# A decoder layer on one core: the 32x32 diagonal blocks of a half inverted in one pass of steps instead of two, in a PSUM bank

## The chip, the cores and the metric

The kernel runs on one core of a Trainium2 chip. The metric is the device time of one execution in microseconds (us), as the median of several runs; a profiled execution stands beside them. The engines are named as in the profile: PE is TensorE, DVE is VectorE, ACT is ScalarE, POOL is GpSimd, SP is SyncE, which issues most DMAs. SBUF is the on-chip memory with 128 partitions, PSUM the accumulation memory with eight banks of 512 fp32 numbers per partition.

## What is computed

One layer of a hybrid decoder over 1024 tokens of 1024 numbers: an input projection, sliding-window attention for one group of heads, a gated DeltaNet for four other heads, an output projection, an MLP and a gated embedding `p @ w_ple_proj`. The change lies in the DeltaNet. Its chunked form needs, for each chunk of 64 tokens and each head, the inverse of a lower triangular matrix with ones on its diagonal:

```python
L = jnp.where(strict, jnp.einsum('bhncd,bhnsd->bhncs', k_beta, k) * decay, 0.0)
eye = jnp.eye(C, dtype=q.dtype)                       # C = 64
T = lax.linalg.triangular_solve(eye + L, jnp.broadcast_to(eye, L.shape),
                                left_side=True, lower=True)
u = jnp.einsum('bhncs,bhnsd->bhncd', T, v_beta)
w = jnp.einsum('bhncs,bhnsd->bhncd', T, k_beta * jnp.exp(g)[..., None])
```

and then a scan over the chunks with a state per head. `p @ w_ple_proj` depends on nothing of the layer, and is used only at its end.

## The kernel before

The 1024 tokens are two halves of 512, each of four token tiles of 128. Matmuls in fp32 are made of three passes of a rounded format, for which each weight tile is split: ScalarE rounds it (L219), VectorE or GpSimd subtracts (L220).

**How the order comes about.** The program is written as Python generators: a long filler (`projections`, L1083 on, PE's large matmuls) and tasks (`prepare`, `attend`, `chain`, `pairs`) that are woken by events and by due times in a count of PE time. That gives the order in which instructions are written down. The scheduler of the framework then makes a fixed order for each engine, by a model of the durations and with that order as the priority. On the chip each engine works off its own queue in that order and waits by semaphores. `take(k)` (L157) gives a PSUM bank of a ring: "g" has three for large matmuls; "d" has four and "e" one in the first stage, two and three afterwards (L1187).

**The recurrence's part.** `chain(hb, ...)` (L1170) runs for each half: `scalars`, `norms` (the scale `bb` of the blocks goes to a DRAM buffer BD and comes back as `bS`, L702 to L705) and `pre` (L717). For each token tile, `pre` makes the decay (POOL `rD` L722, ACT `et` L733, POOL L735), two products per head on PE, and multiplies them by `et` into `ka` (DVE, L749). The 32x32 diagonal blocks of the first product go to a DRAM buffer LD (L755). After tile 1 and after tile 3 it calls `inverse(s, g)` (L760) for a group of two tiles.

`inverse` handles 32 blocks (2 tiles x 4 heads x 4 blocks). The 128 partitions are 32 blocks x 4 parts of 8 columns of the inverse. It zeroes XS and sets ones (POOL, L769 and L773), loads LS, the blocks (SP, L772, four DMAs), scales LS by `bS` (DVE, L775) and takes 31 steps of forward substitution. A step is a product into `tp` (L779) and a subtraction from XS (L780), both on DVE over (31 - j) x min(j + 1, 8) elements a partition; each needs the instruction before it. Then XS goes to a DRAM buffer XD (SP, L782, four DMAs). Group 0 has tiles LS and XS of its own, group 1 uses the tiles `rD` and `et` again, which are free after the last tile's `ka`. The two groups' steps can be in flight at the same time.

`merge(s, tt)` (L784), one per token tile, begins when both groups of the half have been written down: `load_x` brings the inverses from XD into Xt (two buffers, SP, L839), DVE transposes them (L800), and PE and DVE join pairs of 32x32 inverses to 64x64. `prep` and `scan` follow, the scan with two groups of heads and a state `St`; its results `oS` (L947) go to PE to be transposed (L106).

**What PE has beside it.** In the second half of the stage PE's filler is the last projection, then `embed` (L1047, `p @ w_ple_proj`, 192 matmuls of 128x256, started as a spare while the first half's scan is awaited), then `w_out(0)` (384 such matmuls), which needs the first half's scan but nothing of the second half, then `w_out(1)`, the first part of which needs no scan.

Of the kernel before, what the change touches and what calls it, by code (L numbers as in the profile page):

```python
# [10 lines left out]
F32 = mybir.dt.float32  # L11
F32R = mybir.dt.float32r
AF = mybir.ActivationFunctionType
ALU = mybir.AluOpType
# [4 lines left out]
P = 128  # L19
# [90 lines left out]
def bc(ap, dim, n):  # L110

    a = ap.unsqueeze(dim)
    shape = list(a.shape)
    shape[dim] = n
    return a.to_broadcast(shape)
# [3 lines left out]
def hybrid_block(ctx, tc, t, out):  # L119
# [493 lines left out]
    def dt_(shape, name, p=dn, bufs=None, dt=F32):  # L613
        return p.tile(shape, dt, tag=name, name=nm(name), bufs=bufs)
# [51 lines left out]
    def norms(s, q, k):  # L666

        b, free = yield from take("e")
        sq = dt_([P, 2, 4, P], "rD", bufs=1, dt=F32R).bitcast(F32).rearrange("p i h c -> p i (h c)")
        xs = [(sel[i], x[:, h, 3:], h) for i, x in enumerate((q, k)) for h in range(4)]  # L670
        for j in range(9):
            if j < 8:
                A.activation(sq[:, j % 2], xs[j][1], AF.Square)
                yield 0.99
            if j:
                m, _, h = xs[j - 1]
                T.matmul(b[h * 32:h * 32 + 32, :], m, sq[:, (j - 1) % 2],
                         start=j <= 4, stop=j > 4)
        sb = dt_([P, 4, P], "et", bufs=1).rearrange("p h c -> p (h c)")
        A.copy(sb, b)  # L680
        free()
        yield 2.38
        b, free = yield from take("e")
        for tt in range(4):
            T.transpose(b[:, tt * P:(tt + 1) * P], sb[:, tt * P:(tt + 1) * P], ident)
        for i in range(2):
            V.tensor_scalar(s["ss"][:, i].rearrange("p (t h) -> p t h", t=4),
                            b.rearrange("p (t h x) -> p x t h", t=4, h=4)[:, i], EPS, None,
                            op0=ALU.add)
        free()  # L690
        w = lambda name: dt_([P, 16], name, bufs=2)
        rk2, rk, c2d, cc, bb = w("rk2"), w("rk"), w("c2d"), w("cc"), w("bb")
        ssq, ssk = s["ss"][:, 0], s["ss"][:, 1]
        V.reciprocal(rk2, ssk)
        V.tensor_tensor(bb, s["beta"], rk2, op=ALU.mult)
        yield 3.17
        b, free = yield from take("e")
        T.transpose(b[0:16, 0:P], bb, ident)
        bT = dt_([16, P], "bT", bufs=1)
        A.copy(bT, b[0:16, 0:P])  # L700
        free()
        SY.dma_start(s["BD"], bT)  # L702
        bS = dt_([P, 2, 32], "bS")
        for x in range(4):
            SY.dma_start(bS[x * 32:x * 32 + 32], s["BD"].rearrange("(g x) (b c) -> (x b) g c", g=2, b=4))  # L705
        G.tensor_tensor(rk, ssk, mhalf, op=ALU.pow)
        sc4 = dt_([P, 4, 2, 2, 2], "sc4", bufs=2)
        v = lambda x: x.rearrange("p (t g h) -> p t g h", t=4, g=2)
        V.tensor_tensor(sc4[:, :, :, 0], v(bb), v(s["eG"]), op=ALU.mult)
        V.tensor_tensor(sc4[:, :, :, 1], v(s["beta"]), v(rk), op=ALU.mult)  # L710
        V.reciprocal(c2d, ssq)
        V.tensor_scalar(c2d, c2d, 1.0 / (128.0 * 128.0), None, op0=ALU.mult)
        G.tensor_tensor(cc, ssq, mhalf, op=ALU.pow)
        V.tensor_scalar(cc, cc, 128.0 ** -0.5, None, op0=ALU.mult)
        s.update(bb=bb, bS=bS, sc4=sc4, c2d=c2d, cc=cc)

    def pre(s, q, k, place):  # L717
# [10 lines left out]
        for tt in range(4):  # L728
            b, free = yield from take("e")
            for i in range(2):  # L730
                T.matmul(b, mgtR, rD[:, i].rearrange("p h c -> p (h c)"), start=i == 0, stop=i == 1)
            et = dt_([P, 4, P], "et", bufs=1)
            A.activation(et, b.rearrange("p (h c) -> p h c", h=4), AF.Exp)  # L733
            free()
            G.tensor_tensor(et, et, bc(mle, 1, 4), op=ALU.mult)  # L735
            if tt < 3:
                rD = decay(tt + 1)
            kap, wait = place(tt)
            for e in wait:
                yield e  # L740
            ka = dt_([P, 2, 4, P], "ka", kap, bufs=4 if kap is dn else 2)
            s["KE"][tt], s["AT"][tt] = ka[:, 0], ka[:, 1]
            sl = slice(3 + tt * P, 3 + (tt + 1) * P)
            yield 3.0
            for j, x in enumerate((k, q)):
                b, free = yield from take("e")
                for h in range(4):
                    T.matmul(b[:, h * P:(h + 1) * P], k[:, h, sl], x[:, h, sl], start=True, stop=True)
                V.tensor_tensor(ka[:, j], b.rearrange("p (h c) -> p h c", h=4), et, op=ALU.mult)  # L749
                free()  # L750
                if j == 0:
                    ld = s["LD"].rearrange("(t h b) (s c) -> t b s h c", t=4, h=4, s=32)
                    for blk in range(4):
                        r = slice(blk * 32, blk * 32 + 32)
                        SY.dma_start(ld[tt, blk], ka[r, 0, :, r])  # L755
                yield 3.02
            if tt % 2:
                inverse(s, tt // 2)

    def inverse(s, g):  # L760


        if g:
            LS = dt_([P, 2, 4, P], "rD", bufs=1, dt=F32R).bitcast(F32).rearrange("p i h c -> p (i h c)")
            XS = dt_([P, 4, P], "et", bufs=1).rearrange("p h c -> p (h c)")[:, 0:256]
        else:
            LS, XS = dt_([P, 1024], "LS", bufs=1), dt_([P, 256], "XS", bufs=1)
        y = slice(g * 32, g * 32 + 32)
        G.memset(XS, 0.0)  # L769
        for x in range(4):  # L770
            d = slice(x * 32, x * 32 + 32)
            SY.dma_start(LS[d], s["LD"][y])  # L772
            G.memset(XS[d, x * 8:256:33], 1.0)  # L773
        LS, X3 = LS.rearrange("p (s c) -> p s c", s=32), XS.rearrange("p (j i) -> p j i", j=8)
        V.tensor_tensor(LS, LS, bc(s["bS"][:, g], 1, 32), op=ALU.mult)  # L775
        for j in range(31):
            n, m = 31 - j, min(j + 1, 8)
            tp = dt_([P, 192], f"tp{g}", bufs=1)[:, 0:n * m].rearrange("y (k i) -> y k i", k=m)
            V.tensor_tensor(tp, bc(LS[:, j, j + 1:32], 1, m), bc(X3[:, 0:m, j], 2, n), op=ALU.mult)  # L779
            V.tensor_tensor(X3[:, 0:m, j + 1:32], X3[:, 0:m, j + 1:32], tp, op=ALU.subtract)  # L780
        for x in range(4):
            SY.dma_start(s["XD"][y, x * 256:x * 256 + 256], XS[x * 32:x * 32 + 32])  # L782

    def merge(s, tt):  # L784

# [347 lines left out]
    DIRECT = {(0, 1), (0, 2), (0, 3), (1, 0), (1, 1)}  # L1133

    x1 = []
    opened = Event()
    pairs_done = ev(2)

# [56 lines left out]
        G.memset(x, 0.0)  # L1195
    z1.append(dt_([P, 4, HB], "z1", dx))
    opened.done = True

    def half(hb, *a):
        left = pairs(s01[hb], hb, *a)  # L1200
# [265 lines left out]
```

## Time and profile before

| | us |
|---|---|
| median of the 3 runs | 1421.25 |
| lowest, highest | 1418.36, 1424.12 |
| the profiled execution: its own time | 1420.29 |
| its span | 1418.5 |

The granted TensorE clock of the profiled execution is 0.985 on average. A row of busy time counts an engine's instructions; gaps of PE are told by the timeline, where [2.59 <-DVE ka L749] behind a row means that the engine stood idle for 2.59 us before it, and that the last thing it waited for was line 749 on VectorE. In the names, `bk` is a PSUM bank and `tp` the steps' product. Two instructions in a row of one engine overlap a little where the second does not need the first. The rows that are used stand two sections below.

### The profile page before, as it was taken

Reading aid. Unit: us, or ns where it says so; the run is one execution under the profiler, and the core shown is the slowest. Engines: PE = TensorE matmul, PEld = TensorE weight load, DVE = VectorE, ACT = ScalarE, POOL = GpSimd, SP = SyncE. Lnnn points to the kernel's source line nnn. Section 1 sums busy time; section 2 is a strip of 40 time slices with the busy share of each in tenths; the row PEclk is TensorE's granted clock in tenths of the full one; section 3 lists DMA queues with packets and bytes.
Section 4 is the critical chain, followed back from the end, with each engine's and each line's share of the span. In section 5 each row is a group of like instructions: output and inputs, shape, how many; then the busy total and the mean of one; then the engine's idle time right before and its main releaser. Section 6 shows DMA issues by size and latency. Waiting matters only on the chain.

```text
span 1418.5 us, 20396 instructions
## 1 busy us (share of the span) xinstructions
PE 1368.2 (96%) x7856; PEld 1163.6 (82%) x7856; DVE 705.8 (50%) x1438; ACT 502.1 (35%) x1029; POOL 498.9 (35%) x500
## 2 busy tenths in 40 slices
PE   8899999899987899999999999999999999999997
PEld 7788778788886899988888888888888888888886
DVE  6786967998579855433223222222222322135543
ACT  6456465444344334433031220312203122043333
POOL 6673636531555435423032230312214122031222
PEclk9999999999999899999999999999999999999999
DMA  6312222222225423321121111211102111133211
GB/s 210 95 46 76 61 53 65 64 73 70 61 58 166 145 67 96 105 68 52 37 68 45 38 48 41 67 45 45 52 30 68 45 51 47 31 118 126 91 45 46
DMA packets 86706, 99.77 MB, mean 70 GB/s; under 512 B 15984, under 2 KB 67744, under 8 KB 86608
## 3 DMA queue, kind: packets, MB, share of 16 engines
q1 hardware_dynamic: 83712, 92.71, 22.0%
q10 hardware_dynamic: 2544, 4.99, 1.1%
q8 instruction: 62, 1.02, 0.3%
q0 software_dynamic: 352, 0.76, 0.2%
q14 instruction: 36, 0.29, 0.1%
HBM read 88.98 MB, written 9.45 MB: 69 GB/s over the span
## 4 chain that ended last, share of the span: by engine, by line
PE 78%; DVE 14%; issue 2%; DMA 2%; ACT 1%; POOL 1%; SPq 1%; DVEq 0%; POOLq 0%; ACTq 0%
PE bk L102 76%; DVE tp L779 2%; DVE cv L412 2%; PE bk L106 2%; DVE XS L780 1%; DMA AT<-in_xT 1%; DVE w L220 1%; DVE s L549 1%; DVE et L780 1%; DVE s L558 1%; DVE H L412 0%; DMA raw<-in_w_in 0%; DVE ka L749 0%; DVE mx L553 0%; DVE pt L569 0%
## 5 line engine op out<-in xcount | busy, mean ns | idle before, releaser
L220 POOL TENSOR_TENSOR w<-raw,w 128x512 fp32r<-128x512 f32 x144 | 193.0, 1343 | 501.4 <-ACT w L219 401.6
L102 PE MATMUL bk<-R,w 128*128 128x256 f32 (+1 forms) x1920 | 355.7, 331 | 0.9 <-DVE xq L404 0.7
L219 ACT CAST w<-raw 128x512 fp32r<-128x512 f32 (+1 forms) x248 | 153.7, 620 | 563.0 <-PE bk L102 366.1
L102 PE MATMUL bk<-aT,w 128*128 128x512 f32 x1536 | 349.6, 389 | 0.0
L102 PEld LDWEIGHTS bk<-aT,w 128*128 128x128 f32 x1536 | 288.5, 188 | 59.9
L102 PEld LDWEIGHTS bk<-R,w 128*128 128x128 f32 x1920 | 287.1, 190 | 42.9 <-issue 6.9
L220 DVE TENSOR_TENSOR w<-raw,w 128x512 fp32r<-128x512 f32 (+1 forms) x104 | 79.9, 768 | 243.6 <-ACT w L219 243.3
L102 PE MATMUL bk<-M,w 128*128 128x512 f32 x768 | 198.8, 394 | 0.0
L102 PEld LDWEIGHTS bk<-M,w 128*128 128x128 f32 x768 | 144.5, 188 | 34.1
L1337 DVE TENSOR_TENSOR H<-bk,H 128x512 f32<-128x512 f32 x96 | 65.0, 690 | 106.0 <-PE bk L102 106.0
L220 POOL TENSOR_TENSOR aT<-Z,aT 128x512 fp32r<-128x512 f32 x32 | 41.5, 1298 | 137.5 <-ACT aT L219 137.5
L102 PE MATMUL bk<-U,w 128*128 128x512 f32 (+1 forms) x384 | 76.3, 345 | 1.6 <-ACT ba L472 1.2
L102 PEld LDWEIGHTS bk<-U,w 128*128 128x128 f32 x384 | 58.5, 188 | 17.9 <-issue 7.3
L102 PE MATMUL bk<-w,U 128*128 128x256 f32 (+2 forms) x384 | 65.0, 323 | 5.9 <-ACT w L219 3.8
L102 PE MATMUL bk<-w,R 128*128 128x256 f32 (+1 forms) x480 | 69.2, 294 | 0.1
L102 PEld LDWEIGHTS bk<-w,U 128*128 128x128 f32 x384 | 56.1, 194 | 12.7 <-ACT w L219 4.4
L102 PEld LDWEIGHTS bk<-w,R 128*128 128x128 f32 x480 | 62.4, 195 | 2.5 <-issue 1.9
L1337 DVE TENSOR_TENSOR AT<-bk,AT 128x512 f32<-128x512 f32 x32 | 21.9, 691 | 59.3 <-PE bk L102 59.3
L555 ACT ACTIVATE s<-s,mx 128x257 f32<-128x257 f32 (+1 forms) x64 | 31.2, 490 | 50.2 <-DVE mx L553 45.8
L102 PE MATMUL bk<-M,aT 128*128 128x512 f32 (+1 forms) x204 | 47.9, 383 | 0.0
L102 PE MATMUL bk<-R,aT 128*128 128x512 f32 (+1 forms) x204 | 47.8, 383 | 0.0
L1286 DVE SCALAR_TENSOR_TENSOR Z<-bk,rsb 128x512 f32<-128x512 f32 x16 | 11.1, 691 | 70.8 <-PE bk L102 70.8
(339 smaller groups left out, 1835.6 us busy)
## 6 DMA issues: line engine op xcount, KB each, us to landing
raw<-in_w_in SPq DMA_DIRECT2D x72, 256.0 KB, 2.8
raw<-in_w_up SPq DMA_DIRECT2D x64, 256.0 KB, 2.7
raw<-in_w_down SPq DMA_DIRECT2D x64, 256.0 KB, 2.8
raw<-in_w_o SPq DMA_DIRECT2D x32, 256.0 KB, 2.9
PD<-po SPq DMA_DIRECT2D x16, 256.0 KB, 2.6
rawg<-in_w_gate SPq DMA_DIRECT2D x16, 256.0 KB, 2.8
pr<-PD SPq DMA_DIRECT2D x8, 512.0 KB, 3.7
AT<-in_xT SPq DMA_DIRECT2D x14, 256.0 KB, 4.5
```

The costliest lines, as they stand in the source:

```text
L102: self.tc.nc.tensor.matmul(o, lh, rh, **k)
L106: self.tc.nc.tensor.transpose(o, x, i)
L219: A.copy(hi, src)
L220: lo_eng.tensor_tensor(lo, src, hi.bitcast(F32), op=ALU.subtract)
L412: V.scalar_tensor_tensor(cv if i < 3 else x[:, 3:], x[:, i:i + HB], cw[:, j, i:i + 1], cv, op0=ALU.mult, op1=ALU.add)
L549: V.tensor_tensor_reduce(out=s[:, i, lo:256], in0=b[:, i, lo:256], in1=amask[:, lo:256], scale=1.0, scalar=NEG, op0=ALU.add, op1=ALU.max, ...
L555: A.activation(s[:, i, lo:257], s[:, i, lo:257], AF.Exp, bias=mx[:, i:i + 1], accum_out=sm[:, i:i + 1])
L558: V.tensor_tensor(s[:, :, lo:256], s[:, :, lo:256], bc(sm, 2, 256 - lo), op=ALU.mult)
L779: V.tensor_tensor(tp, bc(LS[:, j, j + 1:32], 1, m), bc(X3[:, 0:m, j], 2, n), op=ALU.mult)
L780: V.tensor_tensor(X3[:, 0:m, j + 1:32], X3[:, 0:m, j + 1:32], tp, op=ALU.subtract)
L1286: V.scalar_tensor_tensor(r, b, 0.0, rB[hb], op0=ALU.max, op1=ALU.mult)
L1337: V.tensor_tensor(h, bs[m], h, op=ALU.add)
```

## The change

`pre` no longer calls `inverse` after tile 1 and after tile 3, but once, after the last tile. The pass handles all 64 blocks of the half. The partitions are 64 blocks x 2 parts of 16 columns, so a step has (31 - j) x min(j + 1, 16) elements a partition. LS and XS are the tiles `rD` and `et` in both halves. XS is filled in SBUF by POOL, copied by ACT into a PSUM bank, worked on there, and copied back by ACT before it is stored. The bank is one of "d" in the first half and one of "e" in the second (`inv_bank`). The loads of LS are two DMAs of 64 partitions, as are the stores of XS; `bS` comes in two DMAs instead of four.

```diff
-        bS = dt_([P, 2, 32], "bS")
-        for x in range(4):
-            SY.dma_start(bS[x * 32:x * 32 + 32], s["BD"].rearrange("(g x) (b c) -> (x b) g c", g=2, b=4))
+        bS = dt_([P, 32], "bS")
+        for x in range(2):
+            SY.dma_start(bS[x * 64:x * 64 + 64], s["BD"].rearrange("y (b c) -> (y b) c", b=4))
...
-            if tt % 2:
-                inverse(s, tt // 2)
-
-    def inverse(s, g):
-
-
-        if g:
-            LS = dt_([P, 2, 4, P], "rD", bufs=1, dt=F32R).bitcast(F32).rearrange("p i h c -> p (i h c)")
-            XS = dt_([P, 4, P], "et", bufs=1).rearrange("p h c -> p (h c)")[:, 0:256]
-        else:
-            LS, XS = dt_([P, 1024], "LS", bufs=1), dt_([P, 256], "XS", bufs=1)
-        y = slice(g * 32, g * 32 + 32)
+        yield from inverse(s)
+
+    def inverse(s):
+
+
+        rD = dt_([P, 2, 4, P], "rD", bufs=1, dt=F32R).bitcast(F32)
+        LS = rD.rearrange("p i h c -> p (i h c)")
+        XS = dt_([P, 4, P], "et", bufs=1).rearrange("p h c -> p (h c)")
         G.memset(XS, 0.0)
-        for x in range(4):
-            d = slice(x * 32, x * 32 + 32)
-            SY.dma_start(LS[d], s["LD"][y])
-            G.memset(XS[d, x * 8:256:33], 1.0)
-        LS, X3 = LS.rearrange("p (s c) -> p s c", s=32), XS.rearrange("p (j i) -> p j i", j=8)
-        V.tensor_tensor(LS, LS, bc(s["bS"][:, g], 1, 32), op=ALU.mult)
+        for x in range(2):
+            d = slice(x * 64, x * 64 + 64)
+            SY.dma_start(LS[d], s["LD"])
+            G.memset(XS[d, x * 16:512:33], 1.0)
+        b, free = yield from take(inv_bank[0])
+        A.copy(b, XS)
+        LS, X3 = LS.rearrange("p (s c) -> p s c", s=32), b.rearrange("p (j i) -> p j i", j=16)
+        V.tensor_tensor(LS, LS, bc(s["bS"], 1, 32), op=ALU.mult)
         for j in range(31):
-            n, m = 31 - j, min(j + 1, 8)
-            tp = dt_([P, 192], f"tp{g}", bufs=1)[:, 0:n * m].rearrange("y (k i) -> y k i", k=m)
+            n, m = 31 - j, min(j + 1, 16)
+            tp = dt_([P, 256], "tp", bufs=1)[:, 0:n * m].rearrange("y (k i) -> y k i", k=m)
             V.tensor_tensor(tp, bc(LS[:, j, j + 1:32], 1, m), bc(X3[:, 0:m, j], 2, n), op=ALU.mult)
             V.tensor_tensor(X3[:, 0:m, j + 1:32], X3[:, 0:m, j + 1:32], tp, op=ALU.subtract)
-        for x in range(4):
-            SY.dma_start(s["XD"][y, x * 256:x * 256 + 256], XS[x * 32:x * 32 + 32])
+        A.copy(XS, b)
+        free()
+        for x in range(2):
+            SY.dma_start(s["XD"][:, x * 512:x * 512 + 512], XS[x * 64:x * 64 + 64])
```

## Rows read from the trace of the kernel before

**Rows 1.** The page: busy time, share of the span and instructions of each engine.

```profile
PE 1368.2 (96%) x7856; PEld 1163.6 (82%) x7856; DVE 705.8 (50%) x1438; ACT 502.1 (35%) x1029; POOL 498.9 (35%) x500
```

**Rows 2.** Windows of 20 us: start:end, length, busy time of each engine (instructions), granted clock.

```profile
440.00:460.00 20.00, 11.20 (x80) 10.13 (x81) 19.26 (x63) 9.26 (x25) 8.77 (x13) 0.95 0.62 189
460.00:480.00 20.00, 15.45 (x132) 14.23 (x131) 17.70 (x41) 6.92 (x14) 10.19 (x9) 0.63 0.46 138
```

**Rows 3.** The chain of waits, shares by line: of the whole span, then from 440 to 475 us.

```profile
by line: PE bk L102 75.9%; issue 2.5%; DVE tp L779 2.1%; DVE cv L412 1.7%; PE bk L106 1.7%; DVE XS L780 1.2%; DMA AT<-in_xT 1.2%; DVE w L220 0.9%; DVE s L549 0.7%; DVE et L780 0.7%; DVE s L558 0.6%; DVE H L412 0.4%; DMA raw<-in_w_in 0.4%; D
...
by line: DVE tp L779 25.0%; PE bk L102 19.1%; DVE et L780 16.1%; issue 7.8%; DVE XS L780 7.6%; DVE rD L775 3.2%; DVE vn L908 3.1%; DVE oS L947 2.3%; DVE XT L800 2.3%; DVE ka L816 2.2%; PE bk L106 2.1%; DVE ka L749 1.7%; DVE X L821 1.2%; DVE
```

**Rows 4.** Timeline of TensorE: start, duration, instruction, count [idle before, releaser].

```profile
251.51 1.16 PE L102 MATMUL bk<-H 128*128 128x128 f32 x8 [2.59 <-DVE ka L749]
...
269.64 0.63 PE L106 MATMUL bk<-con,s 128*128 128x128 f32 x4 [2.26 <-DVE mx L549]
...
442.15 0.71 PE L102 MATMUL bk<-vn,ka 128*128 128x128 f32 x4 [2.62 <-ACT oS L911]
...
458.02 0.74 PE L106 MATMUL bk<-con,oS 128*128 128x128 f32 x2 [4.71 <-DVE oS L947]
...
463.39 1.12 PE L102 MATMUL bk<-XT,ka 64*64 64x64 f32 x16 [2.09 <-DVE XT L800]
...
471.55 4.51 PE L102 MATMUL bk<-w,AT 128*128 128x256 f32 x23
...
487.34 3.09 PE L102 MATMUL bk<-w,AT 128*128 128x256 f32 x24
```

**Rows 5.** Windows around both inversions, VectorE instructions that use `tp` alone (L779 and L780).

```profile
240.00:335.00 95.00, 39.90 (x124) 0.98 0.27 68
405.00:490.00 85.00, 51.16 (x124) 0.88 0.44 131
```

**Rows 6.** Timeline of VectorE: two dependent pairs of steps, each start and duration.

```profile
245.45 0.18 DVE L779 TENSOR_TENSOR tp<-LS,XS 128x31 f32<-128x31 f32 x1
...
245.66 0.19 DVE L780 TENSOR_TENSOR XS<-XS,tp 128x31 f32<-128x31 f32 x1
...
459.25 0.36 DVE L779 TENSOR_TENSOR tp<-rD,et 128x192 f32<-128x192 f32 x1
...
459.64 0.36 DVE L780 TENSOR_TENSOR et<-et,tp 128x192 f32<-128x192 f32 x1
```

**Rows 7.** Single lines: shortest/median/longest ns, first and last start, shapes.

```profile
L779 DVE TENSOR_TENSOR tp<-LS,XS x62: 157/274/1359, 245.4 to 453.5; 128x112 f32<-128x112 f32 x4, 128x31 f32<-128x31 f32 x2, 128x60 f32<-128x60 f32 x2, 128x87 f32<-128x87 f32 x2
...
L558 DVE TENSOR_TENSOR s<-s,sm x32: 415/693/1765, 90.0 to 293.8; 128x512 f32<-128x512 f32 x28, 128x256 f32<-128x256 f32 x4
...
L404 DVE TENSOR_TENSOR H<-bk,rsb x12: 676/682/692, 66.9 to 210.5; 128x512 f32<-128x512 f32 x12
...
L992 DVE TENSOR_SCALAR z<-bk,rstd x8: 468/474/484, 402.7 to 431.4; 128x256 f32<-128x256 f32 x8
...
L219 ACT CAST w<-raw x248: 596/621/700, 25.8 to 1292.3; 128x512 fp32r<-128x512 f32 x120, 128x528 fp32r<-128x528 f32 x4
```

**Rows 8.** Timeline of VectorE on the second half's way from `ka` to the merge.

```profile
431.99 0.68 DVE L749 TENSOR_TENSOR ka<-bk,et 128x512 f32<-128x512 f32 x1
...
448.97 1.22 DVE L775 TENSOR_TENSOR rD<-rD,bS 128x1024 f32<-128x1024 f32 x1
...
453.82 0.16 DVE L780 TENSOR_TENSOR XS<-XS,tp 128x8 f32<-128x8 f32 x1
...
462.90 0.43 DVE L800 STREAM_TRANSPOSE XT<-Xt 128x256 f32<-128x256 f32 x1
...
492.64 0.45 DVE L800 STREAM_TRANSPOSE XT<-Xt 128x256 f32<-128x256 f32 x1 [3.68 <-DMA Xt<-XD]
```

**Rows 9.** Timeline of SP's DMA queue: the second half's last load for the steps.

```profile
438.38 1.74 SPq L772 DMA_DIRECT2D rD<-LD  x4
```

**Rows 10.** Window, TensorE's matmuls that read `AT` (embed) alone.

```profile
461.00:491.00 30.00, 14.94 (x96) 0.77 0.47 141
```

More of the change, by code (lines that the diff above doesn't have):

```diff
@@ L1135, in hybrid_block @@
     x1 = []
+    inv_bank = ["d"]
     opened = Event()
@@ L1197, in hybrid_block @@
     opened.done = True
+    inv_bank[0] = "e"
     def half(hb, *a):
```

## The prediction

> **What bounds the kernel now.** The page comes first: TensorE is busy for 1368.2 of 1418.5 us, so there are 50 us of gaps [rows 1]. Next come windows of 20 us. From 440 to 480 TensorE works 26.64 of 40 us while VectorE works 36.97, and the granted clock falls to 0.63 [rows 2]. So in this stretch VectorE leads and TensorE follows. The chain of waits says with what. Over the whole span it runs through matmuls (75.9% on L102), with 2.1%, 1.2% and 0.7%, together 57 us, on the two lines of the inversion's steps, L779 and L780; from 440 to 475 steps are 48.7% of it (25.0, 16.1 and 7.6) and matmuls 19.1% [rows 3]. TensorE's timeline then gives each gap and its releaser: 2.59 us behind `ka` and 2.26 behind `mx` in the first half's inversion, 2.62 behind the scan's `oS` of ScalarE, 4.71 behind that of VectorE and 2.09 behind the merge's transpose in the second's [rows 4]. None of the first four waits for an inverse; three wait for a VectorE instruction that stands in line among steps, and the third for ScalarE, which in turn follows VectorE in the scan but also has casts in its queue.
>
> **Why the steps are so dear.** The steps of one half, 124 instructions, take 39.9 us in the first half and 51.2 in the second [rows 5]. Undisturbed they would be quicker. A dependent pair of 192 elements starts 0.39 us apart, one of 31 elements 0.21 [rows 6], which gives 1.12 ns an element and 0.175 us fixed. A pass has 31 pairs and, in each of the two lines, the sum over j of (31-j) x min(j+1, 8) = 3156 elements: 62 x 0.175 + 6312 x 1.12 ns = 17.9 us, two passes 35.9. The rest is stretching: the same line takes between 157 and 1359 ns [rows 7]. Which instructions stretch is seen in the lines: L558, with both inputs in SBUF, goes from 0.69 (its median) to 1.77 us, while L404, with one input in a PSUM bank, stays within 676 to 692 ns over 12 of the same 128x512 [rows 7]. The latter is the form that both step lines take after the change: L779 reads LS from SBUF and X from the bank, L780 reads X from the bank and `tp` from SBUF.
>
> **The change part by part.**
>
> Steps: 62 a half instead of 124. With min(j+1, 16) a line has 4776 elements, so a half costs 62 x 0.175 + 9552 x 1.12 ns = 21.6 us, if nothing stretches. VectorE is relieved of about 39.9 - 21.6 = 18 us in the first half and 30 in the second, and of one scaling of LS (1.2 us, [rows 8]) in each. As a chain of its own this pass is longer than one of the old ones (17.9), and it starts only after the last token tile's `ka`.
>
> The bank: no row shows VectorE writing to PSUM. Reading from it costs nothing more by L404 against L558's median (682 against 693 ns). The nearest form with a dearer fixed part is L992, 474 ns for 256 elements [rows 7]: 474 - 256 x 1.12 = 187 ns, 12 more than a step. A gain isn't excluded, as the bank lies elsewhere than the other input. So between -12 and +12 ns a step, -0.7 to +0.7 us a half; I take 0. Against the change speaks a table in the Trainium skill (VectorE: DVE Perf Modes, the section on the TRN2 errata): 120 cycles fixed with a PSUM source, 58 with SBUF. By that a step costs 65 ns more, an estimate from that page, 4 us a half, and X comes 4 us later; the forecast below would be 1415. L404 here shows no such surcharge.
>
> Copies into the bank and out: ScalarE, 0.62 us each by L219's 128x512 casts [rows 7], 1.2 us a half, on the way of X. The copy out is a new wait on ScalarE: behind it stand weight casts (L219) and the scan's copies, so TensorE waits in turn if the pass ends later than the order of the queues assumes. The price is 0 if the order is right, and up to the delay itself.
>
> A bank is held for the pass, one of four "d" in the first half (attention shares them) and one of three "e" in the second (merge and prep share them). The gap behind `mx` [rows 4] is a score that VectorE had not read, not a missing bank; 0 to 2.3 us, I take 0.
>
> DMAs: LS loads 16 to 4, X stores 16 to 4, bS loads 8 to 4. SP issues four of them in 1.74 us [rows 9], so 28 fewer relieve SP of 12 us in all. Each is twice as large (bS aside), beside engines that don't wait for them: 0. POOL's memset grows from 256 to 512 columns, and eight short ones become four: 0, ahead of the pass, hidden behind the load of LS.
>
> What the relief gives: the gaps behind queued steps go, that through ScalarE by half: 2.59 + 2.26 + 1.31 + 4.71 = 10.9 us. The clock: at 471.55 23 matmuls took 4.51 us, at 487.34 24 took 3.09, so the low level costs 23 x (0.196 - 0.129) = 1.5 us [rows 4]; with the idle time before it, I take that as gone. Together 12.4 us.
>
> What is late next: the second half's merge. Its tiles 0 and 1 get X now from the first pass, which ends at 453.8; the transpose runs at 462.90, and that of tile 2 at 492.64 [rows 8]. After the change all come from one pass. The last `ka` is at 431.99; the load of LS is issued at 438.38 [rows 9] and the scaling, which waits at 448.97 behind steps [rows 8], can run at about 440. From there 1.2 + 21.6 + 1.2 for copies + 9 for store, load and transposing (453.8 to 462.9) give 473, with some other VectorE work in between (I take 5) 478. So tile 0 comes 10 to 15 us later; tiles 2 and 3 no longer wait for a second pass, which I price at 0. TensorE has work to put ahead of it: 96 matmuls of `embed` (14.9 us after 461, [rows 10]) and then the 384 of w_out(0), 49 us at 0.129. I take 2 us for this wait, as now (2.09, although that cover was there).
>
> Sum: 12.4 - 2 = 10.4 us off the profiled execution's 1420.29 (its span 1418.5 and 1.8 around it): 1409.9. The median of the runs, 1421.25, is 1.0 higher, so **1411 us**; the rivals' times are made from the median too.
>
> **The rivals.**
>
> *The merge takes the place of the steps (slower).* The order on each queue is fixed before the run. If the second half's first merge keeps its place on TensorE, behind the second `St` product of the scan, TensorE gets there 6.0 us earlier (1.31 + 4.71) than now (463.39 less 2.09 is 461), at 455, and waits there for X until 473 to 478: 18 to 23 us, with the casts behind ScalarE's copy out held up as well. 20.5 - 12.4 + 1.5 for the clock, low again, is +9.6: **1431 us**. It decides from 12.4 us of such waiting on. For it: TensorE does wait there now, 2.09 us. Against it: `embed` and w_out(0) need nothing of this half, and 64 us of them are at hand.
>
> *Half of it.* Some of the filler goes ahead, and about 10 us of wait remain at the merge or at the end of the second recurrence, whose merges all start later: -12.4 + 10 = -2.4: **1419 us**.
>
> *More goes than the named gaps.* All of TensorE's idle time from 440 to 480 (40 - 26.64 = 13.4) goes, with the 4.85 of the first half and the clock's 1.5: 19.7 us, **1402 us** [rows 2, 4]. For it: VectorE is busy for 92% of this stretch, and 30 us are taken from it. Against: part of the gaps wait for DMAs and ScalarE.
>
> *It doesn't do what it says.* The steps stretch in the bank as they do now: 51.2 x 9552/12624 = 39 us in the second half. VectorE is relieved of 12 us instead of 30, so 5 of the 12.4 are gained, and X comes 17 later, of which I put 6 on TensorE: **1422 us**. Against it stand L404's 676 to 692. For the output, which no row shows in a bank, the Trainium skill (SBUF — State Buffer, "Who interferes with whom") says that only two SBUF inputs, or two-port modes, make VectorE contend with GpSimd; by that it doesn't happen.
>
> **How the numbers follow.** The forecast has 0.50 (own range 1404 to 1416: the smaller gaps of the same kind, and 0 to 5 us of wait at the merge), half of it 0.20, more 0.13, the slower rival 0.11, and that it doesn't do what it says 0.06. From 1398 to 1427 no more than 2 in 10 is outside: most of the slower rival and the ends of the others. A measurement of this kernel can tell about 0.5%, 7.1 us, so faster means below 1414.1: 0.50 + 0.13, less 0.05 for the forecast's upper end and with a little of the half, 0.59. Slower means above 1428.4: 0.10 of the slower rival and of stretched steps. The same: 0.31.
>
> **What would show it.** L779 and L780 with 62 rows each, none above 0.5 us (the longest has 16 x 16 = 256 elements, 0.29 + 0.175), right if they add up to 21 to 23 us a half. TensorE without the gaps behind `ka`, `mx` and `oS`, and with a granted clock near 1 where it was 0.63. The first transpose of the second half some 35 to 40 us behind the last tile's first `ka`, and TensorE's wait in front of its merge: below 5 us for the forecast, about 10 for half, about 20 for the slower rival. Then the place of `embed` and w_out(0) relative to this merge says why. The forecast is wrong if steps are stretched by POOL or by writing to the bank, if ScalarE stands at the copy out with casts behind it, or if attention lacks the bank.

## The result, and the profile after

| | before | after |
|---|---|---|
| median of four runs each, us | 1420.91 | 1398.06 |
| lowest, highest | 1418.36, 1424.12 | 1394.86, 1398.71 |
| span of the profiled execution | 1418.5 | 1396.9 |

The ratio is 0.9834 (95%: 0.9808 to 0.9859): 1.7% faster, some 23 us, where 1411 (10 us) was forecast. The same kernel in a later set of runs gave 0.9814 (0.9798 to 0.983), so sets differ by up to 3 us, and what follows compares ratios, each against runs of the kernel before in the same set.

The page's busy row [rows 1]:

```profile
PE 1362.1 (98%) x7856; PEld 1159.6 (83%) x7856; DVE 664.4 (48%) x1312; ACT 500.2 (36%) x1030; POOL 492.8 (35%) x486
```

TensorE is busy 6.1 us less for the same 7856 matmuls, and idle 15.5 us less (span less busy time: 50.3, now 34.8). Where it was idle is told by TensorE's windows over three stretches: both inversions of the first half, the second half's up to its merges, and the end of the second scan. Columns: start:end, length, busy time (matmuls), granted clock, share and rate of DMA. First the kernel before, then after.

```profile
225.00:345.00 120.00, 112.03 (x941) 0.99 0.28 71
345.00:500.00 155.00, 134.58 (x1128) 0.92 0.37 106
500.00:580.00 80.00, 80.00 (x713) 1.00 0.27 83
```

```profile
225.00:345.00 120.00, 118.73 (x1016) 1.00 0.32 81
345.00:500.00 155.00, 146.24 (x1289) 0.99 0.38 113
500.00:580.00 80.00, 76.56 (x657) 0.94 0.22 72
```

Length less busy time: 8.0, 20.4 and 0 us of idleness before; 1.3, 8.8 and 3.4 after. So 18.4 us of gaps went and 3.4 came back at the end of the scan. The rest is the clock. Over windows of 5 us from 225 to 580, busy time times (1 - granted clock) adds up to 10.4 us before and 5.3 after. Such a window is 470 to 475 before, with 4.49 us at 0.50 (1.2 GHz), which counts 2.2; it follows the gaps of the merge.

Of the stretch that bounded the kernel [rows 2], after:

```profile
440.00:460.00 20.00, 16.11 (x123) 15.71 (x122) 14.13 (x40) 7.87 (x20) 8.33 (x8) 0.91 0.60 192
460.00:480.00 20.00, 20.00 (x172) 19.86 (x170) 12.97 (x35) 8.65 (x18) 11.49 (x9) 1.00 0.34 93
```

TensorE works 36.11 of 40 us instead of 26.64, VectorE 27.10 instead of 36.97. The steps themselves [rows 5, 6, 7]: VectorE's windows over instructions that use `tp`, the two lines (shortest/median/longest ns), and a pair of the largest steps on the timeline.

```profile
240.00:345.00 105.00, 19.47 (x62) 1.00 0.32 82
400.00:520.00 120.00, 19.71 (x62) 0.99 0.46 137
```

```profile
L777 DVE TENSOR_TENSOR tp<-rD,bk x62: 170/313/421, 271.1 to 469.7; 128x112 f32<-128x112 f32 x4, 128x192 f32<-128x192 f32 x4, 128x240 f32<-128x240 f32 x4, 128x31 f32<-128x31 f32 x2
L778 DVE TENSOR_TENSOR bk<-bk,tp x62: 181/319/432, 271.3 to 469.9; 128x112 f32<-128x112 f32 x4, 128x192 f32<-128x192 f32 x4, 128x240 f32<-128x240 f32 x4, 128x31 f32<-128x31 f32 x2
```

```profile
298.64 0.42 DVE L777 TENSOR_TENSOR tp<-rD,bk 128x256 f32<-128x256 f32 x1
299.10 0.43 DVE L778 TENSOR_TENSOR bk<-bk,tp 128x256 f32<-128x256 f32 x1
299.56 0.40 DVE L777 TENSOR_TENSOR tp<-rD,bk 128x240 f32<-128x240 f32 x1
```

No step is above 0.432 us, where the longest was 1.47 before, and a step of 256 elements starts 0.46 us behind the one before: 0.175 + 256 x 1.12 ns = 0.462. So the bank costs these steps nothing, in reading or in writing.

The largest idle times of TensorE now, beside one row without any [rows 4]:

```profile
333.07 0.68 PE L102 MATMUL bk<-XT,ka 64*64 64x64 f32 x16 [0.92 <-DVE XT L800]
...
437.73 0.33 PE L106 MATMUL bk<-con,oS 128*128 128x128 f32 x1 [2.74 <-DVE oS L947]
...
446.91 4.14 PE L102 MATMUL bk<-R,w 128*128 128x256 f32 x20 [3.85 <-ACT po L1070]
...
479.96 0.68 PE L102 MATMUL bk<-XT,ka 64*64 64x64 f32 x16
...
552.78 1.23 PE L102 MATMUL bk<-vn,ka 128*128 128x128 f32 x4 [1.17 <-ACT oS L911]
```

The merge of the second half, at 479.96, has no idle time before it; w_out(0) (`bk<-R,w`), which began at 490.27 before, begins at 446.91 now and runs up to it. The order that the scheduler made for TensorE is another one, too: ahead of this merge stood 96 of `embed`'s 192 matmuls before, and now stand all of them and 240 of w_out(0)'s 384. VectorE's way to this merge [rows 8]:

```profile
422.50 0.68 DVE L749 TENSOR_TENSOR ka<-bk,et 128x512 f32<-128x512 f32 x1
...
432.68 1.23 DVE L773 TENSOR_TENSOR rD<-rD,bS 128x1024 f32<-128x1024 f32 x1 [3.01 <-DMA rD<-LD]
...
469.94 0.18 DVE L778 TENSOR_TENSOR bk<-bk,tp 128x16 f32<-128x16 f32 x1
...
479.19 0.43 DVE L800 STREAM_TRANSPOSE XT<-Xt 128x256 f32<-128x256 f32 x1
```

### The profile page after: what moved, and what is told of

It reads as the page before. It is cut to its first block, busy times and chain, and to the rows that moved or that the text cites. A ratio compares the mean times of both kernels' runs of the same rounds, so it can differ in the third digit from the quotient of the medians.

```text
span 1396.9 us, 20219 instructions
## 1 busy us (share of the span) xinstructions
PE 1362.1 (98%) x7856; PEld 1159.6 (83%) x7856; DVE 664.4 (48%) x1312; ACT 500.2 (36%) x1030; POOL 492.8 (35%) x486
## 4 chain that ended last, share of the span: by engine, by line
PE 71%; DMA 2%; POOL 1%; DVE 1%; issue 1%; ACT 1%; SPq 0%; POOLq 0%; DVEq 0%; ACTq 0%
PE bk L102 69%; PE bk L106 1%; DMA PD<-po 1%; DMA raw<-in_w_proj 0%; DMA rD<-LD 0%; POOL w L220 0%; POOL cc L713 0%; POOL rk L706 0%; DVE Z L1387 0%; ACT oS L911 0%; POOL oss L942 0%; DVE oS L947 0%; POOL AT L220 0%; POOL R L220 0%; ACT Z L1390 0%
## 5 line engine op out<-in xcount | busy, mean ns | idle before, releaser
L220 POOL TENSOR_TENSOR w<-raw,w 128x512 fp32r<-128x512 f32 x144 | 190.8, 1326 | 533.4 <-ACT w L219 433.4
L102 PE MATMUL bk<-R,w 128*128 128x256 f32 (+1 forms) x1920 | 348.3, 330 | 3.9 <-ACT po L1070 3.9
L220 DVE TENSOR_TENSOR w<-raw,w 128x512 fp32r<-128x512 f32 (+1 forms) x104 | 79.0, 759 | 242.0 <-ACT w L219 241.7
L220 POOL TENSOR_TENSOR aT<-Z,aT 128x512 fp32r<-128x512 f32 x32 | 41.6, 1299 | 139.0 <-ACT aT L219 139.0
L102 PEld LDWEIGHTS bk<-w,U 128*128 128x128 f32 x384 | 55.7, 194 | 14.1 <-DVE w L220 3.3
L220 POOL TENSOR_TENSOR aT<-r,aT 128x512 fp32r<-128x512 f32 x32 | 45.1, 1410 | 0.7 <-ACT aT L219 0.7
```

The costliest lines, as they stand in the source:

```text
L102: self.tc.nc.tensor.matmul(o, lh, rh, **k)
L220: lo_eng.tensor_tensor(lo, src, hi.bitcast(F32), op=ALU.subtract)
```

## The experiments

**The two parts taken singly, the load doubled, and the load taken away.** Theory A puts the gain down to VectorE's busy time, in proportion. `one_pass_sbuf` merges the passes but leaves X in SBUF:

```diff
-        b, free = yield from take(inv_bank[0])
-        A.copy(b, XS)
-        LS, X3 = LS.rearrange("p (s c) -> p s c", s=32), b.rearrange("p (j i) -> p j i", j=16)
+        LS, X3 = LS.rearrange("p (s c) -> p s c", s=32), XS.rearrange("p (j i) -> p j i", j=16)
...
-        A.copy(XS, b)
-        free()
```

> The merged pass alone: one pass of 31 steps over all 64 blocks, as in the changed kernel, but X stays in the SBUF tile `et`; no bank, no two copies. Theory A (the gain is VectorE's relief, about 0.42 us of time for each us of step time taken from it: 22.9 us for 91.1 - 39.2): steps of both halves add up to some 52 us, because with both inputs in SBUF they are stretched again by POOL, up to over 1 us for one step; so 39 x 0.42 = 16 us faster than before, ratio 0.988. Rival B (only the merging counts: fewer instructions and DMAs): steps 40 us, ratio 0.983, as the changed kernel. Rival C (only the bank counts): ratio 0.997 to 1.003.

Measured: 1405.71 us, ratio 0.99 (0.9886 to 0.9915), 14 us off; theory A gives 14.7 for the 35.0 us of steps that went. Its steps:

```profile
L775 DVE TENSOR_TENSOR tp<-rD,et x62: 184/320/1444, 269.8 to 473.2; 128x112 f32<-128x112 f32 x4, 128x192 f32<-128x192 f32 x4, 128x240 f32<-128x240 f32 x4, 128x31 f32<-128x31 f32 x2
L776 DVE TENSOR_TENSOR et<-et,tp x62: 185/352/1504, 270.1 to 473.9; 128x112 f32<-128x112 f32 x4, 128x192 f32<-128x192 f32 x4, 128x240 f32<-128x240 f32 x4, 128x31 f32<-128x31 f32 x2
```

The stretching is back, and the two halves' steps take 24.30 + 31.77 = 56.1 us instead of 39.2.

`two_passes_bank` keeps the two passes of the kernel before and adds only the bank:

```diff
         G.memset(XS, 0.0)
...
+        b, free = yield from take(inv_bank[0])
+        A.copy(b[:, 0:256], XS)
-        LS, X3 = LS.rearrange("p (s c) -> p s c", s=32), XS.rearrange("p (j i) -> p j i", j=8)
+        LS, X3 = LS.rearrange("p (s c) -> p s c", s=32), b[:, 0:256].rearrange("p (j i) -> p j i", j=8)
...
+        A.copy(XS, b[:, 0:256])
+        free()
```

> The bank alone: two passes per half as before, each with 8 columns per part, but X of each in a PSUM bank with a copy in and out. Theory A: no step above 0.5 us, steps of both halves 62 to 68 us (four uncontended passes), 25 us less than before, so 25 x 0.42 = 10 us faster, ratio 0.993. Rival B (only the merging counts): 0.998 to 1.003. Rival C (only the bank counts): 0.983.

Measured: 1399.22 us, ratio 0.9853 (0.9839 to 0.9868), 21 us off, twice what A gave. The steps take 29.21 + 29.34 = 58.5 us, about as long as in `one_pass_sbuf`, but the longest is 0.53 us; and the time is 6.5 us below that kernel's. Busy time alone therefore doesn't set the gain: A falls as a proportion. B, which gave nothing for the bank alone, falls too, and so does C, which gave nothing for the one pass alone. With the bank there, merging brings the ratio only from 0.9853 to 0.9834 or 0.9814, 3 to 6 us; the intervals of the first pair overlap. One rival stays open in this run: TensorE's order isn't that of the kernel before. All of `embed` and 32 matmuls of w_out(0) stand ahead of the merge here, so the 21 us are the bank's and the new order's together. `bank_2nd_half`, below, parts the two for the second half.

`double_product` is the kernel after with each step's product issued twice.

> The changed kernel with each step's product instruction issued twice (the same numbers into `tp`), so 31 more VectorE instructions and about 10 us more of the chain in each half. Theory A: 20 us of step time x 0.42 = 8 us slower than the changed kernel, about 1406. Rival D (after the change VectorE no longer sets the pace, what is left are waits on DMAs and ScalarE): 0 to 2 us slower, 1398 to 1400.

Measured: 1413.62 us, ratio 0.9955 (0.9941 to 0.9969), above both theories. VectorE has 58.5 us of steps, none stretched, as many as in `two_passes_bank`, and the kernel is 14 us slower than that one. What differs between the two is how late X is (the second half's first transpose runs at 461.5 there, at 515.3 here) and TensorE's order. About half of the loss is the clock. From 225 to 580 TensorE is idle 9.4 us longer than in the kernel after, and the clock's loss, added up as above, is 14.6 us instead of 5.3. Of these, 8.0 us lie from 360 to 380, behind a gap of 2.24 us in the first half's merge, at 361.06. Two of TensorE's windows there:

```profile
365.00:370.00 5.00, 4.53 (x42) 0.50 0.06 9
370.00:375.00 5.00, 5.00 (x26) 0.50 0.43 116
```

`no_steps` is the kernel after without the 31 steps (`range(0)`): X stays the identity, so the diagonal blocks are not inverted.

> The changed kernel without the 31 steps (X stays the identity; loads, scaling, copies and stores stay). It leaves out the forward substitution. Theory A: 39 us of step time less, the gaps that remain in the two stretches (1.3 + 8.8 + 3.4 us and 5 for the clock) mostly go: 8 to 16 us faster than the changed kernel, 1382 to 1390. Rival D (VectorE no longer sets the pace): 1395 to 1398.

Measured: 1392.73 us, ratio 0.9809 (0.9792 to 0.9825), 4 us below the kernel after by the ratio (0.9834), 1 us by that of its later set (0.9814), and short of what A asked. 39 us of VectorE work and all of X's lateness are worth no more, while other gaps stay: 11.4 us from 345 to 500.

**Which operand has to be in the bank.** `tp_in_bank` merges the passes and keeps X in SBUF, but writes the product to the bank:

```diff
-            tp = dt_([P, 256], "tp", bufs=1)[:, 0:n * m].rearrange("y (k i) -> y k i", k=m)
+            tp = b[:, 0:n * m].rearrange("y (k i) -> y k i", k=m)
```

> One pass as in the kernel after, but the bank holds the product tp, and X stays in SBUF: L776's product then reads two SBUF operands and writes PSUM, the subtraction reads SBUF and PSUM and writes SBUF. Theory R (what makes a step stretch is reading two operands from SBUF beside GpSimd): the product stretches to over 1 us at times, as with SBUF alone, the subtraction stays below 0.55 us; the steps of a half take about the mean of 19.6 and 28 us, and the time is 1400 to 1404 us. Theory O (any operand or output in PSUM takes the instruction out of the contention): neither stretches and the time is 1396 to 1400 us, with two ScalarE copies fewer. Theory W (writing to SBUF is what contends): the subtraction stretches and the product doesn't, 1400 to 1404 us.

```profile
L776 DVE TENSOR_TENSOR bk<-rD,et x62: 193/368/1530, 270.0 to 479.2; 128x112 f32<-128x112 f32 x4, 128x192 f32<-128x192 f32 x4, 128x240 f32<-128x240 f32 x4, 128x31 f32<-128x31 f32 x2
...
L777 DVE TENSOR_TENSOR et<-et,bk x62: 182/318/421, 270.3 to 479.4; 128x112 f32<-128x112 f32 x4, 128x192 f32<-128x192 f32 x4, 128x240 f32<-128x240 f32 x4, 128x31 f32<-128x31 f32 x2
```

Theory R, reading two operands from SBUF, is borne out: the product (two from SBUF, output in the bank) stretches to 1.53 us, the subtraction (one from each, output in SBUF) stays below 0.43. Where the output lies doesn't matter. What it stretches against is seen when VectorE's and GpSimd's timelines of this kernel are laid side by side:

```profile
451.47 0.99 DVE L776 TENSOR_TENSOR bk<-rD,et 128x220 f32<-128x220 f32 x1
...
455.67 1.25 DVE L776 TENSOR_TENSOR bk<-rD,et 128x240 f32<-128x240 f32 x1
...
458.29 0.97 DVE L776 TENSOR_TENSOR bk<-rD,et 128x252 f32<-128x252 f32 x1
```

```profile
450.90 1.30 POOL L220 TENSOR_TENSOR w<-raw,w 128x512 fp32r<-128x512 f32 x1 [2.37 <-ACT w L219]
...
455.35 1.29 POOL L220 TENSOR_TENSOR w<-raw,w 128x512 fp32r<-128x512 f32 x1
457.51 1.46 POOL L220 TENSOR_TENSOR w<-raw,w 128x512 fp32r<-128x512 f32 x1 [0.87 <-ACT w L219]
```

GpSimd's subtractions for the weight split end at 452.20, 456.64 and 458.97; the steps that began during them end at 452.46, 456.92 and 459.26, that is 0.26, 0.28 and 0.29 us later. At 1.12 ns an element their 220, 240 and 252 elements take 0.25, 0.27 and 0.28. So in these rows a step does nothing until GpSimd's instruction is over. The other rows say the same: of the 19 products that began while one of these subtractions had more than 0.2 us to go, 18 end within 0.02 us of its end plus 1.12 ns an element. In the kernel after 28 steps began so, and none is stretched. The Trainium skill (SBUF — State Buffer, "Who interferes with whom") names this pair, a VectorE instruction with two SBUF inputs against a GpSimd instruction that reads SBUF; the rows agree.

The time, 1409.96 us (ratio 0.991, 0.9897 to 0.9924), is above the forecast of R, and so are the steps: 36.41 + 19.31 = 55.7 us, where R gave 47.6. Freeing one of the two lines saved nothing, since the product alone meets GpSimd as often as both lines together did: 19 steps take over 0.3 us more than their elements, 18 in `one_pass_sbuf`, whose time can't be told from this one's.

**Which half.** `bank_2nd_half` leaves X in SBUF in the first half alone (`take` and both copies only where the bank is "e").

> The kernel after, but the first half's X stays in SBUF (no copies in and out); the second half has it in the bank. Between the kernel after (1398.1) and one pass wholly in SBUF (1405.7) lie 7.6 us. Theory A (the stretched steps cost by what is queued behind them, and the second half's scan is the place): most of the 7.6 us comes from the second half, so this run gives 1398 to 1402 us, and TensorE's idle time from 225 to 345 us rises to about 4.8 us as with SBUF alone, since the first half's gaps are its own. Theory H (both halves alike): 1401 to 1403 us. Theory F (the first half's delays carry over to all that follows): 1404 to 1406 us.

TensorE's windows here, then the second of them in `one_pass_sbuf`:

```profile
225.00:345.00 120.00, 114.61 (x966) 0.99 0.29 75
345.00:500.00 155.00, 147.69 (x1326) 0.99 0.38 113
```

```profile
345.00:500.00 155.00, 142.70 (x1240) 0.97 0.37 112
```

Measured: 1398.96 us, ratio 0.9835 (0.9821 to 0.9848), the same as the kernel after within the intervals. The first half's gaps are there again (5.4 us, kernel after 1.3), and yet the time doesn't show them; where they are made up for isn't shown. So the bank pays in the second half, as theory A said here. The run also answers whether the gain is only another order of TensorE's work: of the 7856 matmuls at least 7768 come in the same order here as in `one_pass_sbuf`, and still the bank in the second half brings the ratio from 0.99 to 0.9835. The spans are 7.1 us apart; from 345 to 500 TensorE is idle 7.3 us instead of 12.3, and from 225 to 580 the clock costs 4.7 instead of 6.4.

**Lateness without load.** In `late_x` ScalarE copies X sixteen times more between bank and SBUF before the store:

```diff
+        for x in range(8):
+            A.copy(XS, b)
+            A.copy(b, XS)
         A.copy(XS, b)
```

> The kernel after, with 16 more copies of X between the bank and SBUF on ScalarE before the store, each waiting for the one before: X comes some 10 to 14 us later in each half, VectorE does nothing more, ScalarE about 10 us more a half. With the step's product doubled the time had risen by 15.6 us, and this run parts the lateness of X from VectorE's load. Theory L (X's lateness is what cost there): the end of the recurrence is late, TensorE idles from 500 to 580 us, and the time is 6 to 14 us above the kernel after, 1404 to 1412 us. Theory V (VectorE's load cost): no more than 3 us above, 1398 to 1401 us. If casts for TensorE's weights stand behind the copies on ScalarE, that shows as gaps with a release by L219 or L220.

Windows of TensorE, and the first transpose on VectorE's timeline:

```profile
345.00:500.00 155.00, 143.64 (x1227) 0.98 0.36 111
500.00:580.00 80.00, 68.80 (x663) 0.94 0.19 61
```

```profile
506.26 0.45 DVE L803 STREAM_TRANSPOSE XT<-Xt 128x256 f32<-128x256 f32 x1 [4.74 <-DMA Xt<-XD]
```

Measured: 1410.13 us, ratio 0.9907 (0.9891 to 0.9922), 10 us above the kernel after by the ratio. VectorE's steps are as they were (39.1 us); the transpose is 27 us later, twice the lateness that was meant, as the first half's delay carries over (the second half's last step begins at 481.6 instead of 469.9, before any of its added copies), and from 500 to 580 TensorE idles 11.2 us instead of 3.4. That is what theory L gave, with two reserves: 1.8 us of TensorE's gaps are ended by GpSimd's L220, which follows a cast, and its order is another one again (456 matmuls `bk<-R,w` between 425 us and the merge, 240 in the kernel after). Lateness fits `double_product`'s idle time too (10.6 us from 500 to 580). Together: the second half's recurrence has little room now, and what X loses beyond some 479 comes out partly in time, while what it gains (`no_steps`, first transpose at 434) is worth at most 4 us.

| kernel | ratio | steps, us | longest step, us | first transpose, 2nd half | TensorE idle: 225-345, 345-500, 500-580 |
|---|---|---|---|---|---|
| before | 1 | 91.1 | 1.47 | 462.9 (last tiles 492.6) | 8.0, 20.4, 0 |
| `two_passes_bank` | 0.9853 | 58.5 | 0.53 | 461.5 (479.4) | 2.7, 11.5, 0 |
| after | 0.9834 | 39.2 | 0.43 | 479.2 | 1.3, 8.8, 3.4 |
| `after_again`, the same kernel | 0.9814 | 39.2 | 0.43 | 476.2 | 0.8, 6.7, 4.1 |
| `bank_2nd_half` | 0.9835 | 43.6 | 1.36 (first half) | 475.8 | 5.4, 7.3, 2.2 |
| `one_pass_sbuf` | 0.99 | 56.1 | 1.50 | 481.4 | 4.8, 12.3, 1.8 |
| `tp_in_bank` | 0.991 | 55.7 | 1.53 | 485.7 | 2.8, 12.6, 6.0 |
| `late_x` | 0.9907 | 39.1 | 0.43 | 506.3 | 0, 11.4, 11.2 |
| `double_product` | 0.9955 | 58.5 | 0.43 | 515.3 | 0, 12.3, 10.6 |
| `no_steps` | 0.9809 | 0 | | 434.3 | 0, 11.4, 0 |

The two rows of the kernel after say how much one profiled execution differs from another: 3 us in the transpose and 2 us in the idle time of a stretch. A difference of that size between two other rows is not told from this.

**The gap that is left.** The largest one, 3.85 us at 446.91, is ended by ScalarE's `po`, which fills one of two `cv` buffers. The one pass needs no LS, XS and `tp` tiles of its own in the first half, which leaves SBUF for more buffers. `cv_four` gives that pool four (`bufs=4`).

> The kernel after with four cv buffers of 2 KB instead of two. In the trace of the kernel after the largest gap of TensorE, 3.85 us at 446.91, ended by ScalarE's copy of a partial product po, which waits for a cv buffer whose store to DRAM is still on its way, in a stretch where two loads of 1 MB run. Theory P (the buffers are that wait): the gap goes, with some of the clock's loss behind it, and the time is 2 to 6 us below the kernel after, 1392 to 1396 us. Theory Q (the next thing is late at once: TensorE then stands behind the scan's oS, 2.74 us at 437.73, or meets the merge before X is there): the gap moves and the time is that of the kernel after, 1397 to 1400 us.

Measured: 1395.02 us, ratio 0.9806 (0.9793 to 0.982); the kernel after had 0.9814 in the next set, so no gain can be told. Neither P nor Q fits, since the gap neither goes nor moves: it is 3.04 us (2.4 in `after_again`), and ScalarE's timeline shows what stands before `po`:

```profile
443.26 0.62 ACT L219 CAST w<-raw 128x512 fp32r<-128x512 f32 x1 [4.88 <-DMA raw<-in_w_o]
443.78 0.58 ACT L1070 COPY po<-bk 128x512 f32<-128x512 f32 x1
```

A cast waits 4.88 us for the load of a w_out weight, and `po` is queued behind it. In the kernel after ScalarE stands there for 3.48 us behind such a load and then 0.86 for a store of `po`. The releaser named on TensorE was thus for the most part not the cause but the next in the queue. So the raw weights got more buffers (`wraw`, two until now), with the kernel after beside them:

> The kernel after as it is, to stand beside the two that follow under the same conditions: 1396 to 1400 us, a ratio of 0.983 to 0.985 to the kernel before.

> The kernel after with four buffers for raw weights instead of two (2 KB each a partition more; the room is there because the one pass needs no LS, XS and tp tiles of its own in the first half). With four cv buffers TensorE's largest gap had stayed (3.85 us, then 3.04), and ScalarE stood before it for 3.5 and 4.9 us at a cast that waited for the load of a w_out weight. Theory D (the gap is the late load of the weights, which is issued only when one of two raw buffers is free): the gap behind po near 445 us goes, and the time is 3 to 8 us below the kernel after, as weights come early everywhere. Theory S (the load is late because SP's queue stands at stores of po in front of it): the gap stays at 2.5 to 4 us and the time is within 2 us of the kernel after. Theory C (more loads collide with those the scan needs): 2 to 6 us above.

> The kernel after with three raw buffers and three cv buffers. If the stores of po and the loads of weights are both waits on a buffer, each with one more buffer gives the larger part of both: 1392 to 1396 us, at or below the kernel with four cv buffers. If only one of them is, it lies between the kernel after and the better of the two. If the scheduler's order moves for other reasons than the buffers, no order of the four is to be expected, and the differences stay within 4 us.

> The kernel after with three raw buffers and its two cv buffers. With four raw buffers the ratio to the kernel before was 0.9778, with three of each 0.9768, with four cv buffers alone 0.9806, with the kernel after 0.9814 under the same conditions. If a third raw buffer is what gains (the load of a weight issued one earlier), this run gives 0.976 to 0.979, 1387 to 1392 us. If the third cv buffer is needed as well, since SP's queue holds loads behind stores, it gives 0.980 to 0.982, 1393 to 1396 us.

| kernel | us | ratio |
|---|---|---|
| `after_again` | 1394.99 | 0.9814 (0.9798 to 0.983) |
| `raw_three` | 1392.57 | 0.9809 (0.9796 to 0.9822) |
| `raw_four` | 1389.97 | 0.9778 (0.9763 to 0.9793) |
| `cv3_raw3` | 1387.65 | 0.9768 (0.9751 to 0.9784) |

`after_again` and `cv3_raw3` lie below what was expected of them. TensorE's window from 345 to 500 in `raw_four`, then the last two in `cv3_raw3`, the fastest:

```profile
345.00:500.00 155.00, 151.23 (x1347) 0.98 0.41 125
```

```profile
345.00:500.00 155.00, 154.32 (x1415) 1.00 0.41 127
500.00:580.00 80.00, 73.14 (x561) 0.94 0.18 57
```

`raw_four` changes the raw buffers alone. There the gap behind `po` is gone, 3.8 us are idle instead of 6.7 (`after_again`), and the time is 5 us lower, the intervals apart, as theory D gave: the load of the weights was late for want of a buffer. In `cv3_raw3` only 0.7 us are idle. A third raw buffer without a third `cv` takes the gap away as well (2.7 us idle), but gains nothing that can be told, as from 500 to 580 7.3 us are idle instead of 4.1; with a third `cv`, 0.5% below the kernel after, 7 us. SP's queue holds the weight loads and the stores of `po` in one order, which fits, but which of the two waits it is was not parted further. What is left, 6.9 us from 500 to 580, is the end of the second scan.

## Why the prediction was right in kind and too small

**What it says of the steps holds.** 62 rows a line, none above 0.5 us, no surcharge of the bank (the one worked out from the table of the Trainium skill, VectorE: DVE Perf Modes, section on the TRN2 errata, an estimate of 65 ns a step, isn't there). A half's steps add up to 19.5 and 19.7 us busy, and with the 0.03 to 0.04 us between them to the 21.6 that were worked out. VectorE was relieved of 20.4 and 31.5 us (18 and 30 forecast). That it doesn't do what it says falls: `one_pass_sbuf` shows about what that would have been (it has no copies), 1405.7, not 1422.

**The term that failed is the relief: 10.9 us of gaps counted, 18.4 gone.** It was added up from single rows of TensorE's timeline: four gaps, one of them at half. The view that groups TensorE's waits by releaser, 225 to 580 us of the kernel before (us in total, times, longest), has more of the same kind:

```profile
PE bk L106 <- DVE oS L947: 9.4, 4, 4.7
PE bk L102 <- DVE XT L800: 2.7, 2, 2.1
PE bk L102 <- ACT oS L911: 2.6, 1, 2.6
PE bk L102 <- DVE ka L749: 2.6, 1, 2.6
PE bk L106 <- DVE mx L549: 2.3, 1, 2.3
PE bk L102 <- DVE X L821: 1.9, 1, 1.9
PE bk L102 <- DVE kd L859: 1.9, 1, 1.9
PE bk L102 <- DVE St L932: 1.1, 1, 1.1
```

After:

```profile
PE bk L102 <- ACT po L1070: 3.9, 1, 3.9
PE bk L106 <- DVE oS L947: 3.6, 2, 2.7
PE bk L102 <- ACT oS L911: 1.2, 1, 1.2
...
```

Only 4.71 of the 9.4 us behind the scan's `oS` was in the sum, and none of what `XT`, `X`, `kd` and `St` held. Not all of this was relief from the steps. Of the second half's, `X` and the longer gap behind `XT` stood behind stretched steps (of 1.12, 1.31 and 1.27 us) in VectorE's queue, but TensorE also has w_out(0) ahead of this merge now, and how much each did isn't parted. `St` stood among steps that weren't stretched, and the gap behind `kd`, at 389.58, lies before the half's first step at 410.56. Against this stand two gaps that were not foreseen: 3.85 us behind `po`, already taken off in the 18.4, and 3.4 us at the end of the scan.

**The clock was priced at 1.5 us and gave 5.1.** The prediction took one group of 23 matmuls at 1.2 GHz. But the clock was down in several places, 425 to 430 and 460 to 475 among them, each behind gaps that then went.

**The merge: 2 us priced, none taken there.** The sum had a slip here: a wait "as now" (2.09 us) is in the time before already, so keeping it costs nothing, and the sum's own terms give 1409 for the median. The time of the second half's transpose was forecast as 473 to 478 and is 479.19 (476.21 in `after_again`). It came about otherwise: the last tile's first `ka` is at 422.50, 9.5 us earlier than before, and the transpose 56.7 us behind it, not 35 to 40, as the pass takes 36 us among the scan's instructions instead of 21.6 + 5. That TensorE doesn't wait is due to w_out(0) from 446.91 on, the cover that the prediction named; the slower rival and half of it fall, since the merge did not keep its place. The price of late X turned up elsewhere, at the end of the scan; `late_x` shows that beyond this point it is real.

**ScalarE and the bank.** The copies took 0.59 and 0.58 us in the second half (0.62 forecast), and no gap stands behind them; no gap shows a wait for the bank either.

Taken together (span): 18.4 us of gaps gone, less 3.4 new ones, and 5.1 of the clock are 20.1 of the 21.6. Of the rest 0.5 is idle time outside the three stretches; where the other 1.0 lies isn't parted. The nearest of the stated cases was that more goes than the named gaps, 1402. In part that was luck: it had all 13.4 us from 440 to 480 go, where 9.5 went (11.7 from 345 to 500), and it had the same 1.5 for the clock, and 4.85 for the first half, where 6.7 went.

Why the bank alone gives 21 us and the one pass alone 14, and both together 23, is shown in part: the one pass takes away load but makes X later, the bank takes away stretching and makes nothing later. Each of the two has an order of TensorE's work of its own besides; at nearly the same order only the bank in the second half was measured. How much of the 3 to 6 us between `two_passes_bank` and the kernel after is lost to lateness was not measured by itself.

## What to carry to other kernels

An instruction that stretches holds up whatever is queued behind it on its engine, too: add up the waits by releaser over the whole stretch, small ones too, before pricing a relief, and add the clock over all windows in which it is down. Where a scheduler fixes the order of the work, compare the orders in two traces before putting their difference down to the edit; a pair with the same order tells more. Here one input in PSUM freed a VectorE tensor_tensor from GpSimd, and it was the inputs that counted, so put the operand that both instructions of a step read there. Where several passes become one, see what the later result will be waited for, and use the SBUF that is saved: here more buffers for weights and stores gave a further 0.5%.

## What the runs showed of the hardware

A VectorE tensor_tensor with both inputs in SBUF, begun while GpSimd subtracts 128x512 from SBUF, ended after GpSimd's end plus its own elements at 1.12 ns each, in 18 of 19 cases of `tp_in_bank` to within 0.02 us; the longest step took 1.53 us. With one input in PSUM the longest of the same shapes was 0.43 us, whether the output was in SBUF or PSUM, and writing 256 elements to PSUM took 0.43 us against 0.42 to SBUF. In `two_passes_bank` one such step of 128 elements took 0.53 us; why isn't shown. Behind gaps of 2 to 5 us TensorE was granted 1.2 GHz for a while: 0.50 from 460 to 475 us before, and 0.50 from 365 to 375 in `double_product`.
